# A hybrid attention and SSD layer on one core: a second place for q and k, more places for attention, and other planned delays behind DMA transposes

## The chip, the core and the metric

The kernel runs on one core of a Trainium2 chip. The metric is the device time of one execution in microseconds. A core has TensorE (PE, with its weight loads shown as PEld), VectorE (DVE), ScalarE (ACT), GpSimd (POOL) and SyncE (SP), which in this kernel issues most DMAs. Each engine takes its instructions in the order of the built program.

## What is computed

One layer for 1024 prompt tokens and 8 x 16 sample tokens (1152 in all, width 1024), cut to what matters:

```
h    = rms_norm(x, norm_g) * (1 + scale) + shift
q, k, v, z_att, z_ssd, xbc, dt, gates = split(h @ w_in)
q, k = rms_norm(q), rms_norm(k)                    # 16 heads of 64
o    = softmax(q k^T / 8 + bias, band of 8 chunks of 64 and the own) v
att  = (o * silu(z_att)) @ w_att_proj
y    = ssd_scan(silu(conv(xbc)), dt, ...)          # 32 heads of 64, state 128
ssd  = group_rms_norm(y * silu(z_ssd)) @ w_ssd_proj
out  = x + gate * ((sigmoid(g1) * att + sigmoid(g2) * ssd) @ w_out)
```

The new k and v rows, convolution rows and states are outputs too. Sample tokens attend to a cache of 512 rows and to their own 16.

## The kernel before, in words

**Precision.** Large products are made of f16 halves: an operand is split into a high and a low half, and a product is three matmuls (high x high, high x low, low x high). `dense` (L397, matmuls at L412, L413, L415) makes 128 output channels of 1152 tokens in three groups of 384; each group is 8 x 3 matmuls. `dense_tok` (L451, matmuls at L465 to L467) does the same with tokens on the partitions, for q, k and v of two heads at once.

**Order of the work.** A program in Python writes the instructions of all engines in one order. Its pieces are generators, and `run` (L796) steps through them: a list of dense generators is the backbone, and between its steps the `urgent` and `paced` generators put in softmax, SSD and preparation. A planned clock (`clock`, in ns, counted from rough costs) decides when a generator may go on: `pause(t)` and `until(t)` hold it until the planned clock has come that far. These pauses set places in the queues; they are no waits of the chip. A scheduler behind it can still move single instructions, except those in `late(...)`. What an instruction really needs is held by semaphores.

**Memory.** All tiles lie in one arena of columns. `set_layout` cuts stretches of it into places with a tag, and layouts of different stages overlap. `walloc` takes a free place, or gives up its turn until there is one. So the number of places of a tag also sets how far the plan runs ahead. Tags touched here:

- `raw`: loaded weight parts of 1024 columns (`w_ahead`, L308, loads up to four ahead); `w`: the halves of a split weight.
- `Q`: q and k of a unit by tokens; `S`: places of 640 columns for a block's probabilities and for what its transpose reads, and for bias and k; `q`, `d`, `k`: small tiles.
- `L_V`: f16 halves of v; `L_MORE`: further places at the arena's end (from E0) for the `T` tiles of the SSD stage, overlapping `L_V` and the extra `S` places of attention.

**Attention** (`attention(u)`, L884) runs for 8 units of two heads. `dense_gen` takes the `Q` place, projects q, k, v, and then makes the next unit's gate. `prelude` norms q and k on GpSimd and transposes them on TensorE. `prompt` goes through 8 blocks of 128 queries in rounds: scores (L1115), running minima of the negated scores (L1013, DVE), exponentials (L1010, ACT), then `turn` (L1026): the probabilities become a high and a low half (L1045, L1046, DVE) and two DMA transposes (L1052, SP). After `TURN` planned ns `weigh` (L1060) may put the product with v (L1070) into TensorE's queue. `sample` (L1145) does the same for sample tokens with a copy into planes (L1189, ACT), one DMA transpose (L1190), and a copy back (L1192, DVE), which stands `pause(TURN)` behind the transpose; its product is L1201.

**SSD** (`ssd(p)`, L1399) runs for 16 pairs of heads. Its x goes through the same three steps: L1475 (ACT), L1477 (DMA transpose), L1479 (DVE), the last `pause(TURN + 1000)` behind the transpose. Then come states (L1525), outputs (L1553, L1573) and new states (L1598). Dense work of the next pairs runs beside it. The first SSD projections (`head_dense`) follow the last attention unit in the backbone; they take their tiles from places that attention's layout leaves free, and from `L_MORE`.

**The tail** multiplies by the output weights; nothing of it is changed.

A second version of the whole layer, `general_kernel`, runs only if the value ranges of the inputs call for it; it reads `TURN` too, and did not run in the profiled execution.

Of the kernel before, what the change touches and what calls it, by code (L numbers as in the profile page):

```python
# [16 lines left out]
P = 128  # L17
D = 1024
KT = D // P
NP = 1024  # L20
NB = 8
NS = 16
NT = NP + NB * NS
# [12 lines left out]
GATED = (0, 1, 2, 5, 6, 9, 10, 11, 13, 14)  # L36
BIG = -1e30

TURN = 9000

COLS = 53184
QCOLS = 1024
# [15 lines left out]
HCOLS = COLS - 1280  # L58
# [81 lines left out]
def trunk_kernel(ctx: ExitStack, tc: tile.TileContext, h, again):  # L140
# [8 lines left out]
    arena = Arena(base, HCOLS)  # L149
# [13 lines left out]
    fixed = [0]  # L163
# [9 lines left out]
    for n, w in PARAMS:  # L173
# [22 lines left out]
    bmask4 = cst[:, C_BM4:C_BM4 + 4]  # L196

    HN = NT // 2
    H0 = fixed[0] + 4 * 1024
    W0 = H0 + 16 * HN  # L200
    V0 = W0 + 6 * 512
    Q0 = V0 + 2 * 4 * NQL
    Z0 = Q0 + 4 * 512
    E0 = Z0 + 2 * 1024 + 5 * NT + 12 * 640 + 4 * 512 + 2 * 256 + 2 * 128 + 3 * 84
    E0 = (E0 + 31) // 32 * 32
    XW = 3 * 288 + 2 * 256
    L_RAW = arena.set_layout(fixed[0], [("raw", 4, 1024)])
    L_H = arena.set_layout(H0, [("h", 16, HN)])
    L_W = arena.set_layout(W0, [("w", 6, 512)])
    L_W3 = arena.set_layout(V0, [("w", 2, 4 * NQL)])  # L210
    L_Q = arena.set_layout(Q0, [("q", 4, 512)])
    L_ATT = arena.set_layout(Z0, [("Q", 1, 16 * P), ("T", 5, NT), ("S", 10, 640), ("U", 2, 640), ("K", 4, 512), ("q", 1, 256), ("d", 1, 256),
                                  ("k", 1, 128), ("p", 1, 128), ("n", 2, 36 + 3 * 16), ("t", 6, 14)])
    L_ATT["Z"] = L_ATT["T"][2:]
    L_SSD = arena.set_layout(Z0, [("X", 1, XW), ("R", 2, 1184), ("t", 8, 36), ("pad", 1, 576), ("T", 9, NT), ("Y", 1, 1184), ("H", 1, 1024),
                                  ("g", 3, G3)])
# [2 lines left out]
    L_SM = arena.set_layout(Z0 + 15 * NT, [("e", 2, 384)])  # L219
    L_START = arena.set_layout(Z0, [("T", 11, NT), ("ada", 5, 1024), ("e", 2, 256)])  # L220
    L_START["ada"] = L_START["ada"] + arena.set_layout(E0, [("ada", 8, 1024)])["ada"]
    L_MORE = arena.set_layout(E0, [("T", 6, 1184), ("H", 1, 1024)])
    L_SSD["H"] = L_SSD["H"] + L_MORE["H"]
    L_V = arena.set_layout(E0, [("v", 4, NP // 2)])
    L_ATT["S"] = L_ATT["S"] + arena.set_layout(E0 + 4 * NP // 2, [("S", 4, 640)])["S"]
    L_ST = rarena.set_layout(0, [("b", 4, P), ("s", 2, P), ("x", 2, 2 * P)])

    def alloc(lay, tag, cols):
# [70 lines left out]
    jobs, parts = [], []  # L299
    wraw, wsplit = {}, {}  # L300
    loaded = [0]
    hold = [False]
# [3 lines left out]
        parts.extend(raw)  # L306

    def w_ahead():  # L308
        while not hold[0] and loaded[0] < len(parts) and len(wraw) < 4:
            b = alloc(L_RAW, "raw", 1024)  # L310
            x = parts[loaded[0]]
            dma(b.ap[:, :x.shape[1]], x)
            wraw[loaded[0]] = b
            loaded[0] += 1
# [309 lines left out]
    v = [sq[1].ap[:, i * 9:(i + 1) * 9] for i in range(4)]  # L624
# [143 lines left out]
    def until(t):  # L768
        while clock[0] < t:
            yield -1.0  # L770

    def pause(t):
        yield from until(clock[0] + t)
# [110 lines left out]
    def attention(u):  # L884
# [130 lines left out]
        def prompt():  # L1015
# [10 lines left out]
            def turn(m):  # L1026
# [22 lines left out]
                for e in range(2):  # L1049
                    yield from until(probs[m] + 1000 + 1400 * e)  # L1050
                    x, at = place[m][e]
                    dma(x.ap[:, at:at + n * P].bitcast(U16).rearrange("p (i k) -> p i k", k=P), ys[e].bitcast(U16), transpose=True)  # L1052
                yield from until(probs[m] + 2400 + TURN)
                turned.add(m)
# [90 lines left out]
        def sample():  # L1145

            yield from ready(lambda: "left" in st)
            kb, qdb, qd = st["sm"]
            qd = qdb.ap.rearrange("p (b c) -> p b c", c=2 * NS)
            ks = kb.ap  # L1150
            v, z = (st[n] for n in ("v", "z"))
            for bg in range(2):
                bs = yield from walloc(lay, "U", 640)
                dma(bs.ap, h["bias_s"][u, bg])
                kcs, vcs = [], []
                for i in range(4):
                    kc = yield from walloc(lay, "K", 512)
                    dma(kc.ap, h["kc"][u, 4 * bg + i])
                    kcs.append(kc)
                p = yield from walloc(lay, "U", 640)  # L1160
                sm_ = yield from walloc(lay, "t", 14)
                yield from pause(4500)
                yield from until(sfree[0])
                ps = pss.tile([P, 2, 512], F32, tag="s", name=nm("s"))
                sv = ps.rearrange("p a c -> p (a c)")
                for i in range(4):
                    rw = slice(32 * i, 32 * i + 32)
                    late(nc.tensor.matmul(ps[rw, 0, :], qd[:, 4 * bg + i], kcs[i].ap, start=True, stop=True, tile_position=(0, 32 * i)))
                for i in range(4):
                    rw = slice(32 * i, 32 * i + 32)  # L1170
                    nc.tensor.matmul(ps[rw, 1, :P], qd[:, 4 * bg + i], ks, start=True, stop=True, tile_position=(0, 32 * i))
                for x in kcs:
                    x.free()
                negated(p.ap, sm_.ap[:, 4:5], sv[:, :640], bs.ap)
                exps([p.ap], sm_.ap)
                nc.vector.reciprocal(sm_.ap[:, 8:9], sm_.ap[:, 6:7])
                nc.vector.tensor_scalar(p.ap, p.ap, sm_.ap[:, 8:9], None, ALU.mult)
                sm_.free()
                bs.free()
                yield 1400  # L1180
                sfree[0] = clock[0] + 1800
                tp = clock[0] + 4000
                for i in range(4):
                    vc = yield from walloc(lay, "K", 512)
                    dma(vc.ap, h["vc"][u, 4 * bg + i])
                    vcs.append(vc)
                pt = yield from walloc(lay, "U", 640)
                yield from until(tp)
                nc.scalar.activation(planes(pt, 0, 5), words(p, 0, 5), AF.Copy)  # L1189
                dma(p.ap.bitcast(U16).rearrange("p (i k) -> p i k", k=P), pt.ap.bitcast(U16), transpose=True)  # L1190
                yield from pause(TURN)
                nc.vector.tensor_copy(words(pt, 0, 5), planes(p, 0, 5))  # L1192
                p.free()
                yield from pause(3000)
                while clock[0] < gfree[0]:
                    yield from until(gfree[0])
                po = pg(P)
                for j in range(5):
                    for i in range(4):
                        mv = vcs[i].ap[:, j * P:(j + 1) * P] if j < 4 else v.ap[:, NP:]  # L1200
                        late(nc.tensor.matmul(po[32 * i:32 * i + 32, :], pt.ap[:, j * P + 32 * i:j * P + 32 * i + 32], mv,  # L1201
                                              start=j == 0, stop=j == 4, tile_position=(0, 32 * i)))
                for x in vcs:
                    x.free()
                pt.free()
                os_ = yield from walloc(lay, "p", P)
                nc.scalar.activation(os_.ap, po, AF.Copy)
                yield 1400
                yield from pause(2500)
                while clock[0] < gfree[0]:  # L1210
                    yield from until(gfree[0])
                pt2 = pg(P)
                nc.tensor.transpose(pt2, os_.ap, ident)
                os_.free()
                pv_ = pt2.rearrange("p (b e s) -> p b e s", e=2, s=NS)
                for e in range(2):
                    hs = slice(e * HD, (e + 1) * HD)
                    c = slice(NP + 64 * bg, NP + 64 * bg + 64)
                    nc.vector.scalar_tensor_tensor(
                        z.ap[hs, c].rearrange("p (b s) -> p b s", s=NS), pv_[hs, :, e, :], 0.5 / SW,  # L1220
                        z.ap[hs, c].rearrange("p (b s) -> p b s", s=NS), ALU.mult, ALU.mult)
                yield 110
            kb.free()
            qdb.free()
            done()
# [173 lines left out]
    def ssd(p):  # L1399
# [62 lines left out]
        def main():  # L1462
# [14 lines left out]
            dma(xd.ap.bitcast(U16).rearrange("p (i k) -> p i k", k=P), xw.ap.bitcast(U16), transpose=True)  # L1477
            yield from pause(TURN + 1000)
            nc.vector.tensor_copy(words(xw, 0, 9), planes(xd, 0, 9))  # L1479
# [306 lines left out]
    w, n = NPART + 2, NPART + 2 + NOPER  # L1786
# [15 lines left out]
def general_kernel(ctx: ExitStack, tc: tile.TileContext, h):  # L1802
# [77 lines left out]

    H0 = 0
    W0 = H0 + 16 * NT
    Z0 = fixed[0] + 2 * 1024
# [731 lines left out]
    def attention(u):  # L2615
# [128 lines left out]
        def prompt():  # L2744
# [9 lines left out]
            def turn(m):  # L2754
# [18 lines left out]
                for e in range(2):  # L2773
                    yield from until(probs[m] + 1000 * e + TURN)
                    (x, at), (y, _) = place[m][e], turned[m][e]
# [91 lines left out]
        def sample():  # L2867
# [6 lines left out]
            for bg in range(2):  # L2874
# [35 lines left out]
                dma(p.ap.bitcast(U16).rearrange("p (i k) -> p i k", k=P), pt.ap.bitcast(U16), transpose=True)  # L2910
                yield from pause(TURN)
                nc.vector.tensor_copy(words(pt, 0, 5), planes(p, 0, 5))
# [208 lines left out]
    def ssd(p):  # L3121
# [62 lines left out]
        def main():  # L3184
# [14 lines left out]
            dma(xd.ap.bitcast(U16).rearrange("p (i k) -> p i k", k=P), xw.ap.bitcast(U16), transpose=True)  # L3199
            yield from pause(TURN + 1000)  # L3200
            nc.vector.tensor_copy(words(xw, 0, 9), planes(xd, 0, 9))
# [456 lines left out]
```

## Time and profile before

| | us |
|---|---|
| median of 3 runs | 1843.87 |
| lowest, highest | 1839.16, 1847.39 |
| the profiled execution's own time | 1841.84 |
| its span in the trace | 1839.7 |
| TensorE busy | 1770.4 (96%) |
| VectorE busy | 1229.7 (67%) |
| ScalarE busy | 958.6 (52%) |
| GpSimd busy | 330.0 (18%) |

The page gives busy time of each engine, then the span in 40 slices of 46 us with the busy share of each slice in tenths, the granted TensorE clock and the DMA share. Groups of instructions follow, each with the idle time of its engine ahead of it and what ended that. A row of waits reads: who waited, for whom, us in total, times, the longest. A row of the timeline reads: start, length, engine, line, operation, output and input, count, and in brackets the idle time before it and what ended it. Matmuls overlap, so their distance from start to start is the price of one, not their length.

By stage: start until 92 us, attention until about 690, SSD until about 1472, then the tail.

### The profile page before, as it was taken

What the parts mean: (1) busy time and instruction counts of PE and PEld (TensorE: products, weight loads), DVE (VectorE), ACT (ScalarE), POOL (GpSimd) and SP (SyncE); (2) the same over time, 40 slices, a digit from 0 to 9 for tenths busy, and PEclk for the clock granted to TensorE, in tenths of its full rate; (3) what the DMA queues carried; (4) which work ended last, traced back from release to release, by engine and by line L of the source; (5) the groups of instructions that cost most, each with busy time, mean ns of one, the idle gap of its engine ahead of it and who ended that gap; (6) DMA issues with size and microseconds to landing.
All of it is one profiled execution on the core that took longest, in us unless ns stands there. A gap on an engine that the chain in (4) does not pass through costs nothing. (4 is left out here: it accounts for less than half of the span.)

```text
span 1839.7 us, 35020 instructions
## 1 busy us (share of the span) xinstructions
PE 1770.4 (96%) x13821; PEld 1105.9 (60%) x13821; DVE 1229.7 (67%) x2327; ACT 958.6 (52%) x1903; POOL 330.0 (18%) x624
## 2 busy tenths in 40 slices
PE   7999999999999969999999999999999999999998
PEld 3655555555555546666666667666666656666664
DVE  6466766767677766777676868677764635887732
ACT  8765645555465547644655566356554613334520
POOL 0232322213123101211312222222222110000000
PEclk9999999999999979999999999999999999999999
DMA  9258778678678665443444445334466952331331
GB/s 382 76 132 215 169 193 202 151 208 195 150 221 189 164 159 150 139 138 112 113 141 120 133 132 176 129 114 112 145 177 208 345 172 99 110 98 50 98 122 54
DMA packets 266566, 284.88 MB, mean 155 GB/s; under 512 B 199628, under 2 KB 200664, under 8 KB 266392
## 3 DMA queue, kind: packets, MB, share of 16 engines
q1 hardware_dynamic: 257432, 253.90, 49.6%
q0 software_dynamic: 8960, 28.65, 4.2%
q8 instruction: 110, 1.80, 0.4%
q14 instruction: 64, 0.52, 0.1%
HBM read 192.70 MB, written 43.66 MB: 128 GB/s over the span
## 5 line engine op out<-in xcount | busy, mean ns | idle before, releaser
L412 PE MATMUL d<-arena 128*128 128x384 f16 x2172 | 709.5, 327 | 3.7 <-DVE arena L1423 3.5
L415 PE MATMUL d<-arena 128*128 128x384 f16 x2172 | 709.2, 327 | 0.0
L413 PE MATMUL d<-arena 128*128 128x384 f16 x2172 | 709.2, 327 | 0.0
L415 PEld LDWEIGHTS <-arena 128*128 128x128 f16 x2280 | 223.1, 98 | 147.7 <-issue 1.8
L412 PEld LDWEIGHTS <-arena 128*128 128x128 f16 x2280 | 223.4, 98 | 144.7 <-issue 6.3
L413 PEld LDWEIGHTS <-arena 128*128 128x128 f16 x2280 | 223.2, 98 | 142.4 <-issue 5.1
L322 ACT ACTIVATE arena<-arena 128x1024 bf16<-128x1024 f32 (+3 forms) x169 | 181.8, 1076 | 144.3 <-DMA arena<-in_wall_dram 122.1
L330 ACT ACTIVATE arena<-arena 128x1024 f16<-128x1024 f32 (+1 forms) x117 | 122.1, 1044 | 175.5 <-PE d L413 149.3
L465 PE MATMUL d<-arena 128*128 128x384 f16 (+1 forms) x568 | 186.6, 329 | 1.9 <-ACT arena L668 1.6
L466 PE MATMUL d<-arena 128*128 128x384 f16 (+1 forms) x568 | 186.4, 329 | 0.0
L467 PE MATMUL d<-arena 128*128 128x384 f16 (+1 forms) x568 | 186.3, 328 | 0.0
L331 DVE SCALAR_TENSOR_TENSOR arena<-arena 128x1024 f16<-128x1024 f32 (+1 forms) x117 | 148.9, 1273 | 53.2 <-ACT arena L330 53.0
L1010 ACT ACTIVATE arena<-arena 128x640 f32<-128x640 f32 (+3 forms) x144 | 100.9, 703 | 122.4 <-DVE arena L1013 122.3
L1452 ACT ACTIVATE arena<-arena 128x128 f32<-128x128 f32 x288 | 88.6, 387 | 50.9 <-DMA arena<-acs_d 50.8
L1264 DVE SCALAR_TENSOR_TENSOR arena<-arena 128x1176 f32<-128x1176 f32 x72 | 104.6, 1453 | 12.2 <-ACT arena L1261 11.6
L1046 DVE SCALAR_TENSOR_TENSOR arena<-arena 128x640 f16<-128x640 f32 (+4 forms) x128 | 87.4, 713 | 0.0
L465 PEld LDWEIGHTS <-arena 128*128 128x128 f16 x576 | 56.3, 98 | 51.6 <-issue 17.5
L938 POOL TENSOR_SCALAR arena<-arena 128x16 f32<-128x16 f32 (+1 forms) x24 | 7.5, 312 | 423.0 <-DVE arena L911 422.1
L467 PEld LDWEIGHTS <-arena 128*128 128x128 f16 x576 | 56.4, 98 | 37.4 <-issue 0.3
L466 PEld LDWEIGHTS <-arena 128*128 128x128 f16 x576 | 56.5, 98 | 35.6 <-issue 2.3
L1514 POOL TENSOR_TENSOR rarena<-rarena,arena 128x256 fp32r<-128x256 f32 x64 | 55.3, 878 | 73.8 <-PE g L1598 50.2
L1534 DVE SCALAR_TENSOR_TENSOR arena<-arena,g 128x64 f32<-128x64 f32 x224 | 46.4, 275 | 32.6 <-ACT arena L1530 30.6
(242 smaller groups left out, 2621.0 us busy)
## 6 DMA issues: line engine op xcount, KB each, us to landing
arena<-in_wall_dram SPq DMA_DIRECT2D x85, 512.0 KB
arena<-acs_d SPq DMA_DIRECT2D x32, 576.0 KB
arena<-in_kc_dram SPq DMA_DIRECT2D x64, 256.0 KB
arena<-in_vc_dram SPq DMA_DIRECT2D x64, 256.0 KB
arena<-in_wada_dram SPq DMA_DIRECT2D x24, 512.0 KB
arena<-in_xT_dram SPq DMA_DIRECT2D x16, 576.0 KB
arena<-eacs_d SPq DMA_DIRECT2D x32, 288.0 KB
gate_d<-arena POOLq DMA_DIRECT2D x48, 192.0 KB, 3.1
```

The costliest lines, as they stand in the source:

```text
L322: keep(nc.scalar.activation(junk[:, :n], x, AF.Square, scale=scale * n ** -0.5, accum_out=sums[:, c:c + 1]))
L330: keep(nc.scalar.activation(hi, x, AF.Copy, scale=scale))
L331: keep(nc.vector.scalar_tensor_tensor(lo, x, scale, hi, ALU.mult, ALU.subtract))
L412: nc.tensor.matmul(ps, hi.r[:, wc], kh.r[:, tok], start=k == 0, stop=False)
L413: nc.tensor.matmul(ps, hi.r[:, wc], kl.r[:, tok], start=False, stop=False)
L415: nc.tensor.matmul(ps, lo.r[:, wc], kh.r[:, tok], start=False, stop=k == nk - 1)
L465: nc.tensor.matmul(ps, kh.r[:, tok], wh, start=k == 0, stop=False)
L466: nc.tensor.matmul(ps, kh.r[:, tok], wl, start=False, stop=False)
L467: nc.tensor.matmul(ps, kl.r[:, tok], wh, start=False, stop=k == KT - 1)
L1010: nc.scalar.activation(p, p, AF.Exp, bias=sm_[:, 4 + e:5 + e], scale=-1.0, accum_out=sm_[:, 6 + e:7 + e])
L1264: nc.vector.scalar_tensor_tensor(yc, r.ap[:, j:j + n], w4[:, i, j:j + 1], yc, ALU.mult, ALU.add)
L1452: nc.scalar.activation(me[e].ap[:, cs], me[e].ap[:, cs], AF.Relu, scale=-1.0, bias=a4[:, c, hds[e]:hds[e] + 1])
```

## The change

Six things, all of places and planned delays:

1. `TURN` goes from 9000 to 6500. The weighing of a prompt block and the SSD copy L1479 are planned 2500 sooner; the sample's copy L1192 gets `TURN + 4000`, 10500 in place of 9000.
2. `raw` places: 3 in place of 4; `w` places: 4 in place of 6 (two pairs of halves in place of three).
3. `Q`: 2 places in place of 1, the second behind the arena's E0.
4. `S`: 12 places in one run, in place of 10 and 4 more behind E0.
5. `q`, `d`, `k`: 2 places each in place of 1.
6. Behind E0, `L_V` and `L_MORE` are laid out anew: `L_MORE` has 7 `T` places in place of 6, of which four lie behind its `H` place, where attention has nothing.

The instructions of all engines, by line and count, stay the same; the order in the queues and the addresses change.

```diff
-TURN = 9000
+TURN = 6500
...
-    H0 = fixed[0] + 4 * 1024
+    NSLOT = 12
+    H0 = fixed[0] + 3 * 1024
     W0 = H0 + 16 * HN
-    V0 = W0 + 6 * 512
+    V0 = W0 + 4 * 512
...
-    L_RAW = arena.set_layout(fixed[0], [("raw", 4, 1024)])
+    L_RAW = arena.set_layout(fixed[0], [("raw", 3, 1024)])
     L_H = arena.set_layout(H0, [("h", 16, HN)])
-    L_W = arena.set_layout(W0, [("w", 6, 512)])
+    L_W = arena.set_layout(W0, [("w", 4, 512)])
...
-    L_ATT = arena.set_layout(Z0, [("Q", 1, 16 * P), ("T", 5, NT), ("S", 10, 640), ("U", 2, 640), ("K", 4, 512), ("q", 1, 256), ("d", 1, 256),
-                                  ("k", 1, 128), ("p", 1, 128), ("n", 2, 36 + 3 * 16), ("t", 6, 14)])
+    L_ATT = arena.set_layout(Z0, [("Q", 1, 16 * P), ("T", 5, NT), ("S", NSLOT, 640), ("U", 2, 640), ("K", 4, 512), ("q", 2, 256), ("d", 2, 256),
+                                  ("k", 2, 128), ("p", 1, 128), ("n", 2, 36 + 3 * 16), ("t", 6, 14)])
...
-    L_MORE = arena.set_layout(E0, [("T", 6, 1184), ("H", 1, 1024)])
+    L_MORE = arena.set_layout(E0, [("T", 3, 1184), ("H", 1, 1024)])
+    n = (HCOLS - E0 - 3 * 1184 - 1024) // 1184
+    L_MORE["T"] = L_MORE["T"] + arena.set_layout(E0 + 3 * 1184 + 1024, [("T", n, 1184)])["T"]
     L_SSD["H"] = L_SSD["H"] + L_MORE["H"]
-    L_V = arena.set_layout(E0, [("v", 4, NP // 2)])
-    L_ATT["S"] = L_ATT["S"] + arena.set_layout(E0 + 4 * NP // 2, [("S", 4, 640)])["S"]
+    L_V = arena.set_layout(E0, [("v", 2, NP // 2), ("pad", 1, 160)])
+    L_V["v"] = L_V["v"] + arena.set_layout(E0 + 1184, [("v", 2, NP // 2)])["v"]
+    L_ATT["Q"] = L_ATT["Q"] + arena.set_layout(E0 + 1184 + NP, [("Q", 1, 2048)])["Q"]
...
-        while not hold[0] and loaded[0] < len(parts) and len(wraw) < 4:
+        while not hold[0] and loaded[0] < len(parts) and len(wraw) < 3:
...
-                yield from pause(TURN)
+                yield from pause(TURN + 4000)
                 nc.vector.tensor_copy(words(pt, 0, 5), planes(p, 0, 5))
```

## What was predicted before the run

> **What bounds the kernel now.** I read the page first, then busy time by stage, then TensorE's waits in the stages that are not full, then the rows of the one hole.
>
> ```profile
> span 1839.7 us, 35020 instructions
> ...
> PE   7999999999999969999999999999999999999998
> ...
> PEclk9999999999999979999999999999999999999999
> ```
>
> TensorE is full in every slice but the first and the sixteenth (644 to 690 us), where the granted clock drops too. By stage (columns: window, length, busy TensorE, weight loads, VectorE, ScalarE, GpSimd, granted clock, DMA share, GB/s):
>
> ```profile
> 92.00:598.00 506.00, 488.68 (x4631) 287.08 (x4630) 358.64 (x954) 283.98 (x691) 134.04 (x273) 1.00 0.75 184
> 598.00:645.00 47.00, 44.03 (x404) 26.46 (x405) 33.44 (x91) 25.92 (x59) 5.42 (x16) 0.96 0.67 159
> 645.00:676.00 31.00, 15.92 (x222) 10.85 (x214) 23.93 (x56) 15.13 (x32) 0.31 (x2) 0.71 0.82 190
> 676.00:690.00 14.00, 14.00 (x87) 7.62 (x85) 3.78 (x9) 3.90 (x6) 1.17 (x2) 0.92 0.38 102
> 690.00:1472.00 782.00, 770.93 (x5751) 513.78 (x5753) 544.67 (x810) 442.42 (x831) 170.75 (x299) 1.00 0.50 152
> ```
>
> So idle TensorE is 17.3 us in seven units of attention (92 to 598), 15.1 us in 31 us at the end of the eighth unit, and 11.1 us in the whole SSD stage. No other engine is near full. The 15.1 us, by what TensorE waited for between 645 and 690 us:
>
> ```profile
> PE g L1070 <- DMA arena<-arena: 9.9, 4, 5.6
> PE g L1070 <- DVE arena L1013: 3.7, 1, 3.7
> PE g L1213 <- DVE arena L1121: 1.3, 1, 1.3
> ```
>
> L1070 weighs V by probabilities that a DMA has transposed. The same stretch in order of time:
>
> ```profile
> 655.44 3.41 PE L1070 MATMUL g<-arena 128*64 128x128 f16 x60 [3.67 <-DVE arena L1013]
> 658.78 0.98 PE L1115 MATMUL s<-arena 64*128 64x320 f16 x6
> ...
> 667.65 0.28 PE L1070 MATMUL g<-arena 128*64 128x128 f16 x1 [5.63 <-DMA arena<-arena]
> 668.99 1.81 PE L1070 MATMUL g<-arena 128*64 128x128 f16 x29 [1.05 <-DMA arena<-arena]
> 673.24 0.31 PE L1070 MATMUL g<-arena 128*64 128x128 f16 x1 [2.44 <-DMA arena<-arena]
> 674.33 1.81 PE L1070 MATMUL g<-arena 128*64 128x128 f16 x29 [0.78 <-DMA arena<-arena]
> 676.07 0.50 PE L412 MATMUL d<-arena 128*128 128x384 f16 x1
> ...
> 678.28 0.33 PE L413 MATMUL d<-arena 128*128 128x384 f16 x1
> ```
>
> From 649 (the row at 649.30, below) to 676 us there is not one dense matmul. The chain scores, softmax, transpose, weighing runs bare. It runs bare because the dense work that follows had no place in the arena until attention gave its own back.
>
> **The change, part by part.** Instruction counts and shapes are equal on every engine; only order and addresses move. All terms below come from the order of the built program, priced by rows.
>
> *The hole.* The tail of TensorE's queue, where Dn is n dense matmuls, the blocks of queries are in brackets, and small groups are left out:
>
> ```
> before  S[6] W[4,5] S[7] W[6,7] D29
> after   S[6] D20 D25 D19 D5 W[4,5] S[7] D18 D4 W[6] D33 W[7] D8 W[7] D29
> ```
>
> (S: L1115, W: L1070.) Twenty-two dense matmuls now stand between the last scores and the weighing of block 6, and 33 and 8 more inside that of block 7. One step of a dense matmul is 0.1625 us:
>
> ```profile
> 648.00 0.33 PE L412 MATMUL d<-arena 128*128 128x384 f16 x1
> ...
> 649.30 0.33 PE L415 MATMUL d<-arena 128*128 128x384 f16 x1
> ```
>
> (eight steps in 1.30). Block 7 needed from 659.56+1.01 = 660.6 to 674.33, 13.8 us. In the new order 22+33+8 dense matmuls (10.2 us), the 30 weighings of block 6 (1 us) and the sample's scores (about 2 us) cover 13.2 of it. Block 6 has 69+22 dense matmuls, 14.8 us, and W[4,5] and S[7] ahead of it; its scores stood right behind the dense row at 649.30 (below), so it needed about 18, until 667.65. The waits go, 14.9 us in these rows and 15.1 by the window: **-15.1**. Ends: -15.1 and -8, if block 7 stays late by half.
>
> The slow clock goes with them. Seven dense steps from 676.07 to 678.28 took 2.21 us where 1.14 is usual; 60 weighings took 3.41 and 29 took 1.81 twice, where an undisturbed unit has these:
>
> ```profile
> 365.75 0.44 PE L1115 MATMUL g<-arena 64*128 64x320 f16 x4
> ...
> 385.09 1.08 PE L1070 MATMUL g<-arena 128*64 128x128 f16 x31
> 386.63 1.00 PE L1070 MATMUL g<-arena 128*64 128x128 f16 x29 [0.46 <-DMA arena<-arena]
> ```
>
> That is 1.1+1.3+1.6 = 4.0 us over. I take **-3**, ends 0 and -4. The Trainium skill, "TensorE: Matmul & The Clock Gate", part 1, says that an idle window of about 3.4 us halves the clock and that about 3.4 us of work restore it: at most 1.7 us lost for each hole. The rows agree in kind (steps of 0.32 us after a hole); by the page the three waits over or near 3 us would cost about 5 us in place of my 4.
>
> What is late next is block 3 of that unit: 73 dense matmuls (11.9 us) and 66 short ones stand between its scores and its weighing, about 14 us, and a chain of this kind took 13.8 (above) to 20.4 (below). I take **+4.5**, ends 0 and +7.
>
> *Attention, units 0 to 6.* With a second place for q and k the next unit's projection runs beside this one's softmax, and the score rounds stand closer. What TensorE waits for there today:
>
> ```profile
> PE s L1115 <- DVE arena L1013: 6.3, 6, 1.3
> PE g L1201 <- DVE arena L1192: 6.1, 6, 1.7
> PE s L1168 <- DMA arena<-in_kc_dram: 2.6, 4, 0.9
> ...
> PE g L1070 <- DMA arena<-arena: 0.8, 2, 0.5
> ```
>
> These are 15.8 of the 17.3 idle us. The worst of the new distances is block 7 of units 1, 3 and 5: 43 dense matmuls (7.0 us) and about 5 us of other work, 12 in all. In unit 3 today its scores end at 365.75+0.44 = 366.2 and its second half is there at 386.6: 20.4 us, and TensorE waits 0.46. If that latency stayed, the new order would wait 8 us. But VectorE does other work inside the chain:
>
> ```profile
> 371.27 2.49 DVE L331 SCALAR_TENSOR_TENSOR arena<-arena 128x1024 f16<-128x1024 f32 x1 [1.72 <-ACT arena L330]
> ...
> 375.01 1.22 DVE L331 SCALAR_TENSOR_TENSOR arena<-arena 128x1024 f16<-128x1024 f32 x1
> ...
> 376.94 0.75 DVE L966 SCALAR_TENSOR_TENSOR arena<-g,arena 128x512 f16<-128x512 f32 x1
> 377.60 0.82 DVE L1013 CUSTOM_DVE_ANT_0 arena<-s,arena 128x640 f32<-128x640 f32 x1
> ```
>
> None of these four stands there in the new order: 1.72+2.49+1.22+0.75+0.82 = 7.0 us less, so 13.4 against 12, a wait of 1.4. Block 3 is alike. Its second transpose stands on SP behind four V loads and a weight load:
>
> ```profile
> 335.29 1.23 SPq L1052 DMA_TRANSPOSE arena<-arena  x1
> 336.61 3.33 SPq L1185 DMA_DIRECT2D arena<-in_vc_dram  x4
> 340.05 0.37 SPq L312 DMA_DIRECT2D arena<-in_wall_dram  x1
> 340.47 1.68 SPq L1052 DMA_TRANSPOSE arena<-arena  x1
> ```
>
> In the new order both transposes come first, 3.9 us sooner, against a distance some 7 us shorter: about 1 us of wait. The sample's copy (L1192) is put 1500 later in the planner's clock:
>
> ```profile
> DVE arena L1192 <- DMA arena<-arena: 54.3, 16, 5.0
> ...
> DVE arena L1479 <- DMA arena<-arena: 32.9, 13, 7.4
> ```
>
> It waits 3.4 us each time now, which blocks VectorE and makes the 6.1 us of L1201; most of that goes. Behind a late weighing stand the next projection's matmuls and their evictions on ScalarE; nothing passes it. GpSimd's norms of q and k move too, with 134 of 506 us busy. I count 3.5 us of waits for each of units 1, 3 and 5, 2 for 2 and 4, 3.7 for 0 and 6 together, 18.2 in place of 17.3: **+1**. Ends: -8 (the L1201 waits and a third of L1115's go, nothing comes) and +31 (today's latencies stay: 8 and 4 us in three units, 5 in two, less 15 of today's 17.3).
>
> *SSD.* Sixteen copies (L1479) are put 2500 sooner. They already wait for their DMA, so VectorE waits up to 16 times 2.5 = 40 us more. Behind each copy stand evictions and weight halves that TensorE needs; in the new order its first need lies 11.7 us or more of TensorE work behind the copy's place, and wait plus work to it come to at most about the same. VectorE is busy 545 of 782 us there. **+1.5**, ends 0 and +20. The work behind a pair also starts sooner, but a stage with 11.1 idle us in 782 can't give much.
>
> *Rings.* One raw weight place less (three) and two split pairs in place of three. A job is 72 dense steps, 11.7 us, so three loads still lead by 35 us, and the pair that is overwritten was read out a job ago: **0**, ends 0 and +6. The cover is that job; without it every split would wait for TensorE.
>
> Sum: -15.1-3+4.5+1+1.5 = -11.1. The profiled execution took 1841.84 (2.1 around its span), which gives 1830.7, so **1831**. The runs' median is 1843.87, 2.0 higher; that difference stays in the range.
>
> **Rivals.** *Given back:* the hole goes, but blocks 3, 4, 5 and 7 wait 3 us more than I count in three units (9 us), or VectorE's longer wait in SSD reaches TensorE with 0.6 us a pair (10 us). For it speaks a unit's round of scores, where VectorE carries 36 us of work in 46, and which becomes some 5 us shorter:
>
> ```profile
> 322.70:369.00 46.30, 44.97 (x439) 26.86 (x439) 36.23 (x109) 27.51 (x72) 10.87 (x17) 1.00 0.70 155
> ```
>
> Against it: the rows above. 1831 and about 10 gives 1841.
>
> *Slower:* the transposes, not their neighbours, make the latency. Then units 1, 3 and 5 wait 8+4 us each and 2 and 4 wait 5 each, 46 us, where 15 of today's go: +31-15.1-3+4.5 = 1859. It decides from the point where block 7's chain stays over about 16 us against its 12. For it speaks the landing in the hole, 663.41 to 667.65 with little beside it:
>
> ```profile
> 663.41 3.49 SPq L1052 DMA_TRANSPOSE arena<-arena  x2
> ```
>
> The Trainium skill, "DMA: Bandwidth & Descriptors", gives a DMA 2.0 us and its bytes at 436 GB/s: 2.75 us for these 320 KB (an estimate from the page). The trace shows 4.2; by the page block 7 would not wait at all, and the sum would be some 4 us lower.
>
> *The filler is late itself:* the dense work in the hole needs its own weights and evictions (L331, L1423) behind the softmax on VectorE, and the hole stays with other names: 1842.
>
> **How the numbers follow.** About 0.5% is what a measurement of this kernel can tell from no change: under 1834.6 is faster, over 1853.1 slower, from the median. Forecast 0.53; given back 0.20 and late filler 0.07 (same); slower 0.20. Low end: all waits of the hole, the clock, and 8 in attention: 1841.8-26 = 1816. High end: the bounds of SSD and half of attention's, 1855. The range 1816 to 1855 leaves out most of the slower case.
>
> **What would show it.** Right: no idle of over 3 us at L1070 in the last unit, dense matmuls between its groups, a granted clock near 1.00 there; L1192's wait under 40 us; L1479's over 50 with TensorE's idle in SSD within 3 us of 11.1. Wrong: L1070 waiting for the DMA in units 1, 3 and 5 by over 5 us each, or L412 waiting for L1423 or L331 in SSD.

## The result, and the profile after

| | before | after |
|---|---|---|
| median, us | 1846.5 | 1860.84 |
| lowest, highest | 1839.16, 1850.92 | 1860.28, 1863.52 |
| the profiled execution | 1841.84 | 1863.18 |
| ratio, 95% interval | | 1.0087 (1.0068 to 1.0105) |

The change makes the kernel slower by 0.9%, some 16 us, where 1831 was forecast. The page of the changed kernel (its lines stand 4 lower in the file, so L1070 is L1074 now, L412 is L416, L1168 is L1172, L1479 is L1483):

```profile
span 1861.4 us, 35026 instructions
...
PE 1776.2 (95%) x13821; PEld 1105.3 (59%) x13821; DVE 1218.9 (65%) x2327; ACT 956.7 (51%) x1903; POOL 346.6 (19%) x624
...
PE   7998999899999988999999999999999999999998
...
PEclk9999999999999998999999999999999999999999
```

The span is 21.7 us longer: TensorE is busy 5.8 us more (1776.2 against 1770.4) and idle 15.9 us more. The one low digit of before is gone, and eights stand in several slices. By the stages of the prediction:

```profile
92.00:598.00 506.00, 479.82 (x4535) 280.33 (x4534) 342.30 (x938) 270.51 (x666) 139.49 (x254) 0.99 0.75 180
598.00:645.00 47.00, 44.65 (x411) 25.32 (x410) 34.10 (x88) 26.31 (x62) 13.67 (x31) 1.00 0.74 186
645.00:676.00 31.00, 29.73 (x297) 19.18 (x295) 24.63 (x56) 18.90 (x37) 1.85 (x5) 1.00 0.64 137
676.00:690.00 14.00, 10.97 (x99) 6.13 (x98) 10.30 (x25) 6.35 (x11) 2.46 (x5) 1.00 0.72 179
690.00:1472.00 782.00, 751.91 (x5609) 501.29 (x5608) 529.89 (x798) 424.27 (x808) 170.89 (x299) 0.98 0.49 148
```

The hole is gone: 1.3 us are idle from 645 to 676, where 15.1 were (3.0 in the 14 us behind, where none were), and the clock is 1.00 there. But idle TensorE is 26.2 us in 92 to 598 (17.3 before), and only 4535 matmuls are done there, 96 fewer; at 506/4631 = 0.109 us for one (a mean over unlike ones) that is about 10 us behind. And it is 30.1 us in 690 to 1472 (11.1 before). By 690 us both kernels have done nearly the same number of matmuls (5342 now, 5344 before): by this count, attention has taken what the hole gave. Behind it 142 fewer are done by 1472. What TensorE waits for, first in 92 to 598, then in 690 to 1472:

```profile
PE g L1074 <- DMA arena<-arena: 12.8, 18, 2.1
PE s L1172 <- DMA arena<-in_kc_dram: 5.2, 4, 1.7
```

```profile
PE d L416 <- ACT arena L1360: 8.4, 2, 7.9
PE d L416 <- ACT arena L1249: 5.2, 3, 2.8
PE g L1577 <- ACT arena L1360: 5.1, 1, 5.1
```

The weighing is busy longer, too:

```profile
L1074 PE MATMUL g<-arena 128*64 128x128 f16 x1440 | 55.5, 221 | 19.7 <-DMA arena<-arena 15.3 <-DVE arena L1017 2.2 <-ACT arena L1341 1.1
```

Before, the same line had this:

```profile
L1070 PE MATMUL g<-arena 128*64 128x128 f16 x1440 | 50.6, 228 | 14.4 <-DMA arena<-arena 10.7 <-DVE arena L1013 3.7
```

The waits for ScalarE in 690 to 1472 are new in size: before, no single wait of TensorE there was over 2.1 us. The largest is now one stretch of 7.9 us at 699.5. ScalarE's queue at that time:

```profile
695.10 1.06 ACT L326 ACTIVATE arena<-arena 128x1024 bf16<-128x1024 f32 x1 [4.86 <-DMA arena<-in_wall_dram]
...
698.82 5.36 ACT L1456 ACTIVATE arena<-arena 128x128 f32<-128x128 f32 x18 [1.50 <-DMA arena<-acs_d]
704.09 1.15 ACT L1460 ACTIVATE arena<-arena 128x1152 f32<-128x1152 f32 x1
705.14 1.84 ACT L1456 ACTIVATE arena<-arena 128x128 f32<-128x128 f32 x6
706.89 0.84 ACT L1360 ACTIVATE arena<-d 128x384 f32<-128x384 f32 x2
```

L1360 empties the PSUM tile that the next dense group (L416) needs. Ahead of it stand a weight part that came late (L326) and the decay preparation of the first SSD pair (L1456, L1460), 8.35 us of work. These are all of SyncE's weight loads (L316) of the stretch:

```profile
652.33 0.33 SPq L316 DMA_DIRECT2D arena<-in_wall_dram  x1
665.25 0.63 SPq L316 DMA_DIRECT2D arena<-in_wall_dram  x1
689.99 0.38 SPq L316 DMA_DIRECT2D arena<-in_wall_dram  x1
710.12 0.33 SPq L316 DMA_DIRECT2D arena<-in_wall_dram  x1
```

They are 13, 25 and 20 us apart, where one dense job lasts 11.7. In the SSD stage it is the same picture at 1107: SyncE's loads of 1087.14 and 1107.68 lie 20.5 us apart, with a transpose between, ScalarE waits 9.1 us and TensorE 5.1:

```profile
1103.70 0.32 SPq L851 DMA_DIRECT2D yb<-arena  x1
1104.12 3.47 SPq L1481 DMA_TRANSPOSE arena<-arena  x1
1107.68 0.53 SPq L316 DMA_DIRECT2D arena<-in_wall_dram  x1
```

```profile
1112.43 1.06 ACT L326 ACTIVATE arena<-arena 128x1024 bf16<-128x1024 f32 x1 [9.10 <-DMA arena<-in_wall_dram]
```

```profile
1117.46 2.05 PE L1577 MATMUL g<-arena 128*128 128x128 f32 x8 [5.08 <-ACT arena L1360]
```

Such distances alone are not the cause, though. The kernel before has them in its SSD stage as well, where no wait of TensorE is over 2.1 us; these two loads follow each other:

```profile
1010.25 0.33 SPq L312 DMA_DIRECT2D arena<-in_wall_dram  x1
1035.85 0.38 SPq L312 DMA_DIRECT2D arena<-in_wall_dram  x1
```

But there four raw places let one more load be ahead.

In attention there is something that no row of waits shows. TensorE in unit 3, the dense matmuls left out:

```profile
333.14 0.30 PE L1074 MATMUL g<-arena 128*64 128x128 f16 x4 [0.74 <-DMA arena<-arena]
...
335.07 1.02 PE L1172 MATMUL s<-arena 128*32 128x512 f32 x2 [1.63 <-DMA arena<-in_kc_dram]
336.02 0.25 PE L1074 MATMUL g<-arena 128*64 128x128 f16 x2
336.19 1.05 PE L1172 MATMUL s<-arena 128*32 128x512 f32 x2
337.17 0.35 PE L1074 MATMUL g<-arena 128*64 128x128 f16 x5
338.08 1.04 PE L1172 MATMUL s<-arena 128*32 128x512 f32 x2 [0.29 <-DMA arena<-in_kc_dram]
...
340.46 0.62 PE L1172 MATMUL s<-arena 128*32 128x512 f32 x1
```

L1172 makes the scores of four samples, each on 32 columns of TensorE of its own (tile_position). Each is f32 and shows as two records. Here the scheduler has put weighings between them, and each takes 1.0 us. Where the four stand beside each other, the eight records take 1.06 us in all (e5 below has the row). In the built order of the changed kernel 7 of the 16 groups are pulled apart, most of them inside a weighing. So this is no new loss by itself: the trace of the kernel before shows 8 apart, six of them by the transposes of q and k.

### The profile page after: what moved, and what is told of

It is laid out like the page before. It is cut to its first block, busy times and chain, and to the rows that moved or that the text cites. A ratio compares the mean times of both kernels' runs of the same rounds, so it can differ in the third digit from the quotient of the medians.

```text
span 1861.4 us, 35026 instructions
## 1 busy us (share of the span) xinstructions
PE 1776.2 (95%) x13821; PEld 1105.3 (59%) x13821; DVE 1218.9 (65%) x2327; ACT 956.7 (51%) x1903; POOL 346.6 (19%) x624
## 4 chain that ended last, share of the span: by engine, by line
PE 42%; DMA 7%; ACT 6%; DVE 5%; issue 3%; POOL 1%; SPq 1%; ACTq 0%; DVEq 0%; POOLq 0%
PE d L416 12%; PE d L417 11%; PE d L419 11%; DMA arena<-acs_d 3%; ACT arena L1456 3%; DMA arena<-arena 2%; PE s L1557 1%; PE g L1529 1%; PE g L417 1%; PE g L419 1%; PE g L416 1%; PE g L1577 1%; DVE arena L1268 1%; ACT arena L1479 1%; DVE arena L1488 1%
## 5 line engine op out<-in xcount | busy, mean ns | idle before, releaser
L416 PE MATMUL d<-arena 128*128 128x384 f16 x2172 | 710.7, 327 | 13.7 <-ACT arena L1360 8.4
L416 PEld LDWEIGHTS <-arena 128*128 128x128 f16 x2280 | 224.0, 98 | 145.3 <-issue 6.4
L326 ACT ACTIVATE arena<-arena 128x1024 bf16<-128x1024 f32 (+3 forms) x169 | 181.8, 1076 | 180.7 <-DMA arena<-in_wall_dram 139.5
L335 DVE SCALAR_TENSOR_TENSOR arena<-arena 128x1024 f16<-128x1024 f32 (+1 forms) x117 | 142.6, 1221 | 67.2 <-ACT arena L334 66.8
L1456 ACT ACTIVATE arena<-arena 128x128 f32<-128x128 f32 x288 | 87.5, 388 | 40.6 <-DMA arena<-acs_d 40.5
L942 POOL TENSOR_SCALAR arena<-arena 128x16 f32<-128x16 f32 (+1 forms) x24 | 11.1, 460 | 431.3 <-DVE arena L915 398.6
L1017 DVE CUSTOM_DVE_ANT_0 arena<-s,arena 128x320 f32<-128x320 f32 (+4 forms) x128 | 58.8, 501 | 38.8 <-PE s L1175 34.3
L1074 PE MATMUL g<-arena 128*64 128x128 f16 x1440 | 55.5, 221 | 19.7 <-DMA arena<-arena 15.3
```

What stands on the lines that cost most here:

```text
L326: keep(nc.scalar.activation(junk[:, :n], x, AF.Square, scale=scale * n ** -0.5, accum_out=sums[:, c:c + 1]))
L335: keep(nc.vector.scalar_tensor_tensor(lo, x, scale, hi, ALU.mult, ALU.subtract))
L416: nc.tensor.matmul(ps, hi.r[:, wc], kh.r[:, tok], start=k == 0, stop=False)
L1456: nc.scalar.activation(me[e].ap[:, cs], me[e].ap[:, cs], AF.Relu, scale=-1.0, bias=a4[:, c, hds[e]:hds[e] + 1])
```

## The experiments

Ratios are to runs of the kernel before on the same chip, with 95% intervals. A difference in us is a difference of ratios times 1845; that of the changed kernel is 1.0087.

**Which half of the change loses it.** The theory on hand was that the shorter delays lose the time; the rivals were the smaller rings, and SSD work that runs ahead of the dense work.

*e1_timing*, the delays alone:

```diff
-TURN = 9000
+TURN = 6500
...
-                yield from pause(TURN)
+                yield from pause(TURN + 4000)
```

> The kernel before with the planned delays alone (TURN 6500, the sample's copy 10500). Theory T (the shorter delays lose time: a product or a copy put closer behind its transpose waits for it, and the work behind waits too): about +15 to +25 us against before, most of it idle TensorE in attention (92 to 598 us, 17 us before) and in SSD (11 us before), with the hole of 15 us at the end of attention still there. Rival R (the smaller rings of weights lose it: ScalarE waits longer for a weight part, and evictions stand behind): within 5 us of before. Rival P (it comes from running the SSD pairs earlier against the dense work, which the new places allow): within 5 us of before.

Measured 0.9987 (0.9976 to 0.9998), 2 us faster: the theory in this plain form falls. But it isn't that nothing happens. L1070's waits in 92 to 645 rise from 0.8 to 9.5 us, and this pays for it:

```profile
L1168 PE MATMUL s<-arena 128*32 128x512 f32 x128 | 19.2, 611 | 0.2 <-issue 0.2
```

In this order 15 of 16 groups are whole, and the 128 records occupy TensorE for 19.2 us. Before, the same line had this:

```profile
L1168 PE MATMUL s<-arena 128*32 128x512 f32 x128 | 36.2, 635 | 5.1 <-DMA arena<-in_kc_dram 2.6 <-issue 2.2 <-DVE arena L1013 0.2
```

17 us less busy and 4.9 less idle, for records of about the same length (611 against 635 ns): they overlap. In the changed kernel the line has 34.4 and 5.8.

*e2_places*, the changed kernel with the delays of before (the diff of e1 reversed).

> The changed kernel with the delays of before (TURN 9000 throughout): the places alone. Theory T: -8 to -15 us against before (the hole filled, nothing lost elsewhere), with idle TensorE in 92 to 598 us near 17 and in SSD near 11. Rivals R and P: 0 to +15 us, with the stretch of about 8 us in which TensorE waits for a gate's eviction on ScalarE at 700 us, and ScalarE's L326 waiting for weights 15 us more than before, as in the changed kernel.

Measured 0.9930 (0.9914 to 0.9947), 13 us faster than before, as the theory had it, with idle TensorE of 27.5 in 92 to 598 against an expected 17 (the profiled run has 15 matmuls more done by 598 than before), and of 16.4 in 690 to 1472 against an expected 11. So neither half loses alone; together they lose 29 us against the places alone.

*e3_ssd_back*, the changed kernel with the SSD copy's delay as before:

```diff
-            yield from pause(TURN + 1000)
+            yield from pause(TURN + 3500)
             nc.vector.tensor_copy(words(xw, 0, 9), planes(xd, 0, 9))
```

> The changed kernel with only the SSD copy's delay as before (10000). Theory T splits: if the loss in SSD (10 us of new idle and some slow clock) is of the copy put closer, this is 8 to 14 us faster than the changed kernel, and SSD's idle falls from 21 to near 11. If the copy has no part in it (rivals R and P), within 4 us of the changed kernel.

Measured 1.0017 (1.0006 to 1.0028), 13 us faster than the changed kernel. The stretch at 700 is unchanged (8.8 us idle in 690 to 736), the SSD stage is cured (12.6 us idle in place of 21.3):

```profile
690.00:736.00 46.00, 37.16 (x287) 24.27 (x285) 24.10 (x30) 31.39 (x71) 4.35 (x9) 0.93 0.56 166
736.00:1472.00 736.00, 723.43 (x5405) 482.82 (x5404) 513.90 (x776) 406.49 (x755) 178.50 (x299) 1.00 0.48 149
```

*e4_rings*, the kernel before with three raw places and two pairs:

```diff
-    H0 = fixed[0] + 4 * 1024
+    H0 = fixed[0] + 3 * 1024
...
-    V0 = W0 + 6 * 512
+    V0 = W0 + 4 * 512
...
-    L_RAW = arena.set_layout(fixed[0], [("raw", 4, 1024)])
+    L_RAW = arena.set_layout(fixed[0], [("raw", 3, 1024)])
...
-    L_W = arena.set_layout(W0, [("w", 6, 512)])
+    L_W = arena.set_layout(W0, [("w", 4, 512)])
...
-        while not hold[0] and loaded[0] < len(parts) and len(wraw) < 4:
+        while not hold[0] and loaded[0] < len(parts) and len(wraw) < 3:
```

> The kernel before with three raw places in place of four and two split pairs in place of three, nothing else. Rival R: +8 to +20 us against before, with ScalarE's L322 waiting longer than 122 us for weights and TensorE's dense matmuls waiting in SSD. Theory T and rival P: 0 to +4 us.

Measured 1.0019 (1.0009 to 1.0030), 3.5 us slower: by themselves, beside the delays of before, the rings cost little. ScalarE's waits for weights rise a little, from 122.1 to 129.7 us.

**What the two halves do to each other.** Each of these is the changed kernel with one edit.

*e5_pack*, the groups kept whole. Issued from the last key block, the four are ready together, and the scheduler leaves all 16 groups whole:

```diff
-                for i in range(4):
+                for i in (3, 2, 1, 0):
                     rw = slice(32 * i, 32 * i + 32)
                     late(nc.tensor.matmul(ps[rw, 0, :], qd[:, 4 * bg + i], kcs[i].ap, start=True, stop=True, tile_position=(0, 32 * i)))
```

> The changed kernel with the sample's four score matmuls (L1172) issued from the last key block to the first, so that the scheduler finds all four ready together and leaves them beside each other in all 16 groups; in the changed kernel 7 of 16 groups are pulled apart by other matmuls. Four beside each other take 1.06 us in all (they use different columns of TensorE), apart 1.0 us or more each. Theory K (the pulled-apart groups cost TensorE time): L1172 busy 34 to about 18 us, its waits for the keys 5 to under 3, so -12 to -20 us against the changed kernel, near 1845. Rival S (only the waits of the weighing for its transposes cost time in attention, and an apart matmul hides beside others): within 4 us of the changed kernel.

Measured 0.9980 (0.9968 to 0.9992), 20 us faster than the changed kernel. The same place in unit 3, and the line's group:

```profile
330.27 1.06 PE L1172 MATMUL s<-arena 128*32 128x512 f32 x8 [1.31 <-DMA arena<-in_kc_dram]
```

```profile
L1172 PE MATMUL s<-arena 128*32 128x512 f32 x128 | 17.1, 603 | 4.8 <-DMA arena<-in_kc_dram 4.2 <-issue 0.5
```

L1172 is busy 17.3 us less; 4682 matmuls are done by 598 in place of 4535. The waits of the weighing do not go down with it, they rise from 15.1 to 22.7 us in 92 to 645, which fits that TensorE now reaches them sooner. The new order also filled 690 to 736 (46.00 busy), so not all of the 20 us is the groups' own.

*e6_raw4*, four raw places again (H0, L_RAW and `w_ahead` as before, `w` at 4).

> The changed kernel with four raw weight places as before. Theory R2 (with work closer together the ring of three is too short: weights come late to ScalarE, and evictions behind them hold TensorE at 700 us and in SSD): -6 to -12 us against the changed kernel, the stretch of 7.9 us at 700 us under 3. Rival (SyncE issues weights late because its queue is held by transposes, whatever the ring): within 4 us, the stretch stays.

Measured 1.0027 (1.0012 to 1.0041), 11 us faster. Attention is as in the changed kernel (4548 matmuls by 598), the rest is cured:

```profile
690.00:736.00 46.00, 46.00 (x354) 30.09 (x352) 25.37 (x33) 31.58 (x66) 5.75 (x13) 1.00 0.63 170
736.00:1472.00 736.00, 724.16 (x5400) 483.71 (x5399) 516.57 (x776) 402.72 (x751) 166.59 (x287) 1.00 0.48 149
```

The stretch at 700 is gone and SSD idles 11.8 us. ScalarE's waits for weights fall little in sum (139.5 to 132.0): it matters where they stand.

*e7_prompt_back*, the prompt's delay alone as before:

```diff
-                yield from until(probs[m] + 2400 + TURN)
+                yield from until(probs[m] + 4900 + TURN)
```

> The changed kernel with only the delay of the prompt's weighing as before (9000); the SSD copy stays 2500 sooner and the sample's copy later. If the loss in attention (the waits at L1074 and the pulled-apart groups) is of this delay: -12 to -18 us against the changed kernel, near 1845, with SSD's idle still near 21. If it is of the sample's later copy: within 4 us.

Measured 0.9949 (0.9935 to 0.9963), 25 us faster, more than expected: 4727 matmuls by 598, L1074's waits there 4.4 us in place of 12.8, and no stretch at 700 (0.3 us idle from 690 to 736). SSD idles 17.1 us. The loss in attention is of the prompt's delay; the later sample copy isn't it. Nor are the groups by themselves: in this trace 6 of 16 are still apart and L1172 is busy 30.6 us. And 8.4 of the 25 us are the idle time in 690 to 736 that went too.

*e8_hole*, the first pair's decay preparation planned later:

```diff
-            yield from pause(7000)
+            yield from pause(7000 + (16000 if p == 0 else 0))
             for e in range(2):
```

> The changed kernel with the decay preparation of the first SSD pair (the relus L1456) planned 16000 later, so that 9 in place of 24 of them and none in place of one exponential stand ahead of the first gate evictions L1360 on ScalarE. Theory Q (TensorE's 7.9 us at 700 us is ScalarE's queue order): the stretch falls by 4 to 6 us, and the time by 4 to 8 with the slow clock behind it. Rival (the weights that ScalarE waits for make it, 4.9 us): the stretch stays over 6 us.

Measured 1.0055 (1.0036 to 1.0074), 6 us faster. In 690 to 736 TensorE is busy 43.09 us in place of 37.24, L416's wait for L1360 there 1.5 in place of 7.9. The weight comes as late as in the changed kernel, but less work stands between it and L1360:

```profile
690.59 1.06 ACT L326 ACTIVATE arena<-arena 128x1024 bf16<-128x1024 f32 x1 [5.19 <-DMA arena<-in_wall_dram]
...
696.25 0.84 ACT L1360 ACTIVATE arena<-d 128x384 f32<-128x384 f32 x2
```

So ScalarE's order made most of this stretch; e6 cures it from the other end.

**Do the terms add.**

*e9_T_places*, the kernel before with the new T places alone:

```diff
-    L_MORE = arena.set_layout(E0, [("T", 6, 1184), ("H", 1, 1024)])
+    L_MORE = arena.set_layout(E0, [("T", 3, 1184), ("H", 1, 1024)])
+    n = (HCOLS - E0 - 3 * 1184 - 1024) // 1184
+    L_MORE["T"] = L_MORE["T"] + arena.set_layout(E0 + 3 * 1184 + 1024, [("T", n, 1184)])["T"]
```

> The kernel before with only the new layout of the further T places behind E0, the fourth of them on lying behind the H place. In TensorE's queue 14, 20 and 54 dense matmuls then stand inside the bare chain at the end of attention. Theory H (the record's term for the hole is right, and was lost elsewhere in the changed kernel): -10 to -16 us against before, TensorE's idle of 15 us in the hole under 4. Rival Q (the filler comes late itself, by ScalarE's or VectorE's queue, wherever it is put): within 5 us.

Measured 0.9921 (0.9898 to 0.9944), 14.6 us faster: the whole gain of the change is in these three lines.

```profile
645.00:676.00 31.00, 28.19 (x346) 17.44 (x343) 26.46 (x58) 16.15 (x33) 1.62 (x3) 1.00 0.82 179
```

*e10_places_raw4_pack* (e2 with four raw places and the order of e5), *e11_prompt_back_raw4_pack* (e7 with both) and *e12_all_raw4_pack* (the changed kernel with both):

> The changed kernel with the delays of before, four raw places and the sample's scores issued from the last key block (12 of 16 groups whole, 11 without it). If the three losses add up: 1831 of the places alone, less 4 to 8 for the ring, less 2 to 5 for the groups, 1818 to 1826. If the ring and the groups cost only beside the shorter delays: within 4 us of 1831.

> The same with the SSD copy 2500 sooner and the sample's copy 1500 later, as in the change (13 of 16 groups whole). If the shorter SSD delay costs nothing once weights come in time: within 3 us of the kernel with the delays of before; if the copy itself blocks VectorE ahead of what TensorE needs: 4 to 10 us slower than it, with SSD's idle 5 us higher.

> The changed kernel with four raw places and whole groups of the sample's scores, all delays as in the change. If ring and groups are separate losses: 1860.8-18.5-11.4, about 1831. If they share one (both fix weights or keys that come late): 1838 to 1843. What stays over the kernels with the prompt's delay of before is then the waits of the weighing, 10 to 20 us.

Measured 0.9946 (0.9925 to 0.9967), 0.9966 (0.9950 to 0.9982) and 0.9934 (0.9913 to 0.9954). The last is the main result: with all its delays the changed kernel is 28 us faster once the ring has four places and the groups are whole, and stands at 1833.5 us, level with e2 and e9. e5, e6, e12 and the change itself are a table of two by two:

| ratio to before | groups apart | groups whole |
|---|---|---|
| three raw places | 1.0087 | 0.9980 |
| four raw places | 1.0027 | 0.9934 |

The groups are worth 20 and 17 us, the ring 11 and 8.5: within the intervals they add. Beside the delays of before (e10 against e2) the same two gain nothing, but this tests the ring alone, since only one more group is whole there (12 in place of 11). e11 is 3.7 us slower than e10, which the intervals can't tell from nothing, with SSD idle 10.6 and 12.7: with weights in time the sooner SSD copy costs nothing that can be told.

**Do the delays lose by themselves.**

*e13_T_timing* (e9 with the diff of e1), *e14_whole* (before with whole groups) and *e15_T_whole* (e9 with the same edit). The order of e5 doesn't make the groups whole beside the delays of before, so e14 and e15 have a pause too:

```diff
                 yield from until(sfree[0])
+                yield from pause(1500)
```

> The kernel before with the new T places and with all three delays of the change, but with its own rings (four raw places, three pairs), one Q place and its own attention places; 15 of 16 groups of the sample's scores are whole. If the loss is of groups and ring, and not of the delays themselves: 1831 to 1836, as the T places alone. If shorter delays lose once the hole is filled, whatever the ring: 1842 to 1850, with L1070 waiting over 20 us for transposes in attention.

> The kernel before with the sample's scores issued from the last key block and planned 1500 later, so that 15 of 16 groups are whole in place of 9; nothing else. If the pulled-apart groups cost as much here as in the changed kernel: L1168 busy 36 to under 21 us and its waits for keys 2.6 to near 0, -10 to -18 us against before. If they cost only in the changed kernel, where they stand inside the weighing of units 1, 3 and 5: within 4 us.

> The new T places and whole groups (16 of 16), with the delays, rings and attention places of before. If the two gains add: -14 of the T places and -10 to -18 of the groups, 1815 to 1823, faster than every kernel so far. If the hole is filled no better because the groups stand later: 1826 to 1834.

e13: 0.9958 (0.9940 to 0.9977), 7 us behind e9 by the ratios (the interval of the difference goes from about 1 to 12), between the two expectations. L1168's line is busy 19.1 us in place of 34.0, and waits of the weighing and of the scores take most of it back. e14 and e15: 1.0124 (1.0101 to 1.0146) and 1.0087 (1.0069 to 1.0106), 23 and 31 us slower than without the edit, where gains or no change were expected. The line fell to 19.0 us as expected, but the pause moved the whole sample chain, and its product then waits for its copy:

```profile
PE g L1202 <- DVE arena L1193: 19.8, 6, 5.1
```

That was 6.1 us. So e14 says nothing clean of what apart groups cost the kernel before; that stays open.

## Why the prediction was wrong, step by step

**The hole, -15.1, and what is late next, +4.5: right.** In e9 the terms -15.1-3+4.5 = -13.6 came alone, at -14.6 (interval -10 to -19). In the changed kernel block 3 of the last unit waits 2.35 us, not 4.5, no idle at L1074 exceeds 3 us there, and dense matmuls stand between the groups.

**The slow clock, -3: right there, but a new stretch pays it again.** Behind the 7.9 us at 699.5 the dense steps take 0.32 us until 711.84, 4.4 us of work at half speed, so 2.2 us lost.

**Attention, +1: the first step that failed.** By 690 us the changed kernel should have been 12.6 us ahead (-15.1-3+4.5+1); it is level. Idle TensorE in 92 to 598 came to 26.2 us, where 18.2 were counted. The waits for transposes came in nearly as sized: in unit 3 L1074 waits 0.74 and 2.07 us where 3.5 were counted, none over 2.4 us, L1192's wait on VectorE fell from 54.3 to 28.0 us, and L1201's from 6.1 to 1.8. Two things were not in the sum. The waits for keys (in_kc) doubled from 2.6 to 5.2 us. And the sentence "instruction counts and shapes are equal; only order and addresses move" was taken to mean that prices stay. They don't: put closer behind its transposes, the weighing keeps TensorE busy for 55.5 us in place of 50.6 (49.5 in e7, with the prompt's delay of before), in 57 runs of matmuls in place of 32. This is of the delay and not of the groups, for e12 has 56.0 with all groups whole. The shorter delays cost attention about 14 us: in the changed kernel 8.9 more of idle TensorE and these 4.9; in e1, from 92 to 645, 8.7 more at L1070, 3.8 at L1201 and 1.5 at L1115. In e1 and e13 whole groups paid for that, in the changed kernel nothing did. The price of L1172, 0.27 us for a sample among its like and 1.0 us alone, is no part of the loss, as its line was busy 36.2 us before and is 34.4 now. It is a saving that the prediction did not see and that the order of the changed kernel misses.

**Rings, 0 (ends 0 to +6): failed.** The cover was named: a job lasts 11.7 us, so three loads lead by 35 us. That takes one load for each job, and loads come in bunches. In 736 to 1472 the kernel before has 13 distances of over 18 us between two loads, the changed kernel 10, e6 16, so the distances are not the loss; with three places, one load fewer has gone out ahead of such a gap. In e6 the loads of 666.2 and 702.1 lie 35.9 us apart, and ScalarE's next part comes 0.5 us late, where it was 4.9 in the changed kernel. That the fourth place works by this lead is argued; its price is measured. The measured value is 8.5 to 11 us beside the new delays and 3.5 beside the old ones (e4).

**SSD, +1.5: failed by where it looked.** TensorE's idle there rose by 19 us, 8.8 of them in the stretch at 700 and 10 behind 736. The distance from the copy to TensorE's first need was counted on VectorE, and L1423 or L331 were to show the harm; L416 waits 0.2 us for L1427, which was L1423. The wait came by ScalarE, whose L326 stood in front of evictions. L1483's own wait rose to 41.4 us only (over 50 was forecast). e3 and e6 each cure the part behind 736 alone: the sooner copy and the shorter ring lose it together. Beside a ring of four the sooner copy costs nothing that can be told (e11).

**The rivals.** "Slower" named 1859, and 1860.8 was measured, but not by its mechanism: block 7 would have waited 8 us in units 1, 3 and 5, and the longest wait of L1074 in these units is 2.07. That the number fits is luck. "The filler is late itself" had the right kind of place, evictions that the dense work needs itself, but VectorE in place of ScalarE. None had the price of an instruction depend on where it stands.

The sum, by the runs: -14.6 for the places, +7 for the delays beside them (e13 against e9), and about +24 for what the rest of the change (rings and attention places) does beside these delays (the change against e13), which whole groups and a fourth raw place take off again. That makes +16.

## What to carry to other kernels

Two changes that are harmless alone can lose together: a smaller ring of buffers leaves less lead where loads come in bunches, and work moved closer needs that lead; test the parts and the pair. When only the order moves, look for instructions whose price depends on what stands beside them, such as matmuls on parts of the columns. And when evictions are on ScalarE or VectorE, list what the new order puts ahead of each on that engine, not only how far TensorE's need is.

## What the runs showed of the hardware

Four 128x32 f32 matmuls on separate columns take 1.06 us together, and 1.02 to 1.05 us each with 128x64 matmuls between them. The Trainium skill, "TensorEngine Tiling (Array Packing)", section "Key Properties", says that different tiles can run in parallel and that a change of the tiling mode drains TensorE. The rows agree with the first; the drain can't be told from them.

After 7.9 idle us the dense steps, 0.1625 us at full clock, took 0.32 us for 4.4 us:

```profile
707.41 0.48 PE L416 MATMUL d<-arena 128*128 128x384 f16 x1 [7.90 <-ACT arena L1360]
707.68 0.53 PE L417 MATMUL d<-arena 128*128 128x384 f16 x1
...
711.52 0.53 PE L417 MATMUL d<-arena 128*128 128x384 f16 x1
711.84 0.46 PE L419 MATMUL d<-arena 128*128 128x384 f16 x1
712.13 0.33 PE L416 MATMUL d<-arena 128*128 128x384 f16 x1
```

The Trainium skill, "TensorE: Matmul & The Clock Gate", part 1, gives about 3.4 us of work for the clock to come back, by a window that runs free of the kernel; here it took 4.4 us.
